# Float32 value products of two heads side by side in an attention stage, with row sums from GpSimd additions and quarter-array ones products

## The chip, the cores and the metric

The kernel runs on one core of a Trainium2 chip. The metric is device time in microseconds (us). Five engines work side by side, each executing its own instructions in order: TensorE (PE, with its weight loads shown as PEld), VectorE (DVE), ScalarE (ACT), GpSimd (POOL) and SyncE (SP, which here only issues transfers). They wait for one another through semaphores.

## The reference

One layer of a streaming encoder: modulation, a norm, one input projection, a depthwise convolution for half of the channels and attention with forget gates for the other half, an output projection, and a gated feed-forward network. There are 2048 prompt frames, and 8 sample streams of 16 frames with 1024 cached frames each. Everything is float32. The attention of the prompt, which the change is about, has 8 heads of 64 and is causal:

```python
def _attend(q, k, v, cum_q, cum_k, q_pos, k_pos):
    s = jnp.einsum('bqhd,bkhd->bhqk', q, k, preferred_element_type=jnp.float32) * (HEAD_DIM ** -0.5)
    s = s + (cum_q[..., :, None] - cum_k[..., None, :])
    mask = k_pos[None, :] <= q_pos[:, None]
    s = jnp.where(mask, s, NEG_INF)
    p = jax.nn.softmax(s, axis=-1)
    return jnp.einsum('bhqk,bkhd->bqhd', p.astype(v.dtype), v)
```

`cum` is the running sum of the log forget values. Queries and keys are normalized per head with large gains, so scores are large and need full float32 accuracy.

## The kernel before

The stages follow one another: input projection of the convolution's and the value's columns (to about 280 us), of queries and keys (to 578 us), the attention with the sample streams' attention woven in (to 1198 us), the output projection (to 1330 us), and the feed-forward network. Large products use fp32r, TensorE's fast reduced-precision form: an operand is split into a high part (ScalarE copies it to fp32r) and the remainder (VectorE or GpSimd subtracts), in `parts_of`, and three products high x high, low x high, high x low give the accuracy.

**Order.** A planner simulates the program and orders each engine's instructions by priority and simulated time. `later` shifts the priority of what is created within it (by `MAXIMA_BY` for the maxima, `BACK_BY` for the background). `after` pins an instruction behind another without a semaphore where both are on one engine. `weave` interleaves generators by the counts given with them.

**Steps.** `STEPS` goes over 4 pairs of heads and, for each, 4 blocks of 512 queries (`qb`). A step has `4 * qb + 4` key blocks of 128; the last four are on the diagonal and are cut to 512, 384, 256 and 128 queries. In all 320 score blocks (a key block, one head).

**A score block** (`attend`, L967 on): scores for 128 keys x 512 queries, transposed, are two fp32r products into one of three PSUM banks `u` (L973, L977): `K1`,`Q1` and `K2`,`Q2` hold the parts of the head's rows in the combinations needed; the second pair also has the gate sums and, in rows 96 to 103, the queries' maxima against -1, so that the product subtracts them. On the diagonal a third product adds the mask (L979). ScalarE takes the exponential into `ef` (L981). `parts_of` (L1160, L1161) splits it into the two parts of `e`; every third subtraction goes to GpSimd, the others to VectorE. The value product (L964) is three fp32r products per head into a bank of its own, of width 128: 64 columns of values and 64 columns of ones, so that the row sums come with it. At the end of a step ScalarE copies sums and values out (L998, L999), takes the inverse of the sums by logarithm and exponential, VectorE refines and multiplies (L1003 to L1005), and the result is stored in `cat_d`.

**Maxima** (`score_maxima`, L909 on): the exponential needs each query's maximum first. A product over 96 rows (L934, banks `cv`, two of them) gives the scores the other way round, VectorE reduces each block (L937), and `spread_maxima` (L945) transposes the result and writes it with the help of a mask `bm` into eight rows of `Q2` (L950). Maxima run ahead of the scores by 32 blocks and more; L974 and L975 pin it.

**Loads**: keys (L889, L891) and queries (L903, L927) by GpSimd's queue, values by SP's (L906), the latter split into two parts.

**Background** (`background`, from the third step on): the norm of the convolution's output (`conv_norm`), then `sample_setup` and eight `sample_batch`es. Their PSUM bank is `lane`; many of their products are plain float32 in column tiles of the array (`tile_position`): 32 columns each, four at a time.

## Time and profile before

| | us |
|---|---|
| median of 3 runs (2818.45 to 2822.88) | 2819.75 |
| the profiled execution | 2814.3 |
| its span, first to last instruction | 2812.5 |

Over the whole span the engines are busy: PE 2718.6 us (97%), DVE 2161.9 (77%), ACT 1428.7 (51%), POOL 503.9 (18%). TensorE's granted clock is 0.983 in the mean.

How to read the rows that follow: a row of groups gives line, engine, operation, output and inputs by tile name, rows x columns of the array for PE, the shape, the count, then busy time in us and the mean of one in ns, and the idle time of that engine ahead of them with what ended it. A timeline row starts with start and length in us; a float32 product appears as two instructions, an fp32r product as one. A row of waits has who waited for whom, the total in us, how often, and the longest. A stage row has the window, its length, then each engine's busy time with its count, the granted clock, the transfer engines' share and GB/s.

### The profile page before, as it was taken

The page shows a single profiled execution, that of the slowest core. Times are in us where ns is not written, and L with a number is a line of the kernel's source. Part 1 is how long each engine was busy: PE and PEld are TensorE (multiplying, and loading weights), DVE is VectorE, ACT ScalarE, POOL GpSimd, SP SyncE. Part 2 cuts the span into 40 slices and gives each one's busy share as a digit, 9 for nine tenths or more (in the row PEclk, how much of TensorE's full clock was granted, in tenths as well). Part 3 has the DMA queues.
Part 4 walks back from the last instruction along what each step waited for, and adds up shares of the span by engine and source line. Part 5 has one row for each costly group of instructions (what it writes and reads, how often), then busy time and mean ns, then how long its engine had stood idle before and what let it go on. Part 6 is the DMA issues. An engine that isn't in the chain of part 4 may idle for free. (4 is left out here: it accounts for less than half of the span.)

```text
span 2812.5 us, 48566 instructions
## 1 busy us (share of the span) xinstructions
PE 2718.6 (97%) x16536; PEld 2515.7 (89%) x16536; DVE 2161.9 (77%) x4235; ACT 1428.7 (51%) x2812; POOL 503.9 (18%) x685
## 2 busy tenths in 40 slices
PE   7999999999989999999999999999999999999999
PEld 6999988866667777698999989999999999999999
DVE  2798898989888787546397989877887778666765
ACT  4443323357776777744354446444554446555552
POOL 3454411243333222214201110000000000000000
PEclk9999999979999999999999999999999999999999
DMA  8753657673334766365576869866786769788883
GB/s 325 249 192 107 191 209 267 182 204 109 101 95 128 203 179 189 130 215 179 181 259 209 294 215 308 268 221 218 233 287 214 226 190 319 244 284 257 271 255 116
DMA packets 389960, 599.24 MB, mean 213 GB/s; under 512 B 47136, under 2 KB 250048, under 8 KB 387664
## 3 DMA queue, kind: packets, MB, share of 16 engines
q1 hardware_dynamic: 375248, 570.73, 62.8%
q0 software_dynamic: 14464, 25.42, 3.9%
q8 instruction: 130, 2.13, 0.3%
q14 instruction: 118, 0.97, 0.1%
HBM read 421.97 MB, written 174.08 MB: 212 GB/s over the span
## 5 line engine op out<-in xcount | busy, mean ns | idle before, releaser
L1456 PE MATMUL z<-rT,rW 128*128 128x360 f32 (+1 forms) x8316 | 1383.3, 328 | 5.5 <-ACT rW L1160 1.4
L1456 PEld LDWEIGHTS z<-rT,rW 128*128 128x128 f32 x8316 | 1378.7, 188 | 8.1 <-ACT rW L1160 2.4
L1160 ACT ACTIVATE rW<-rR 128x512 fp32r<-128x512 f32 x714 | 434.4, 617 | 386.8 <-PE z L1456 272.1
L1161 DVE TENSOR_TENSOR rW<-rR,rW 128x512 fp32r<-128x512 f32 x714 | 479.5, 676 | 154.5 <-ACT rW L1160 151.3
L700 DVE SCALAR_TENSOR_TENSOR cv<-cu,cpar,cv 128x384 f32<-128x384 f32 x580 | 311.6, 614 | 2.8 <-ACT cv L698 2.8
L964 PE MATMUL pv<-e,V 128*128 128x512 f32 (+3 forms) x960 | 268.9, 388 | 14.1 <-DVE e L1161 6.3
L964 PEld LDWEIGHTS pv<-e,V 128*128 128x128 f32 x960 | 167.9, 194 | 71.7 <-DVE e L1161 14.6
L937 DVE TENSOR_REDUCE M<-mx 128x1 f32<-128x512 f32 (+2 forms) x320 | 188.7, 603 | 50.2 <-PE mx L934 31.7
L981 ACT ACTIVATE ef<-s 128x512 f32<-128x512 f32 (+3 forms) x320 | 167.1, 532 | 116.7 <-PE s L979 47.1
L512 PE MATMUL z<-hqx,wqh 128*128 128x384 f32 (+1 forms) x768 | 196.6, 333 | 1.0 <-DVE logf L347 1.0
L1160 ACT ACTIVATE rT<-traw 128x360 fp32r<-128x360 f32 (+1 forms) x315 | 149.1, 501 | 91.7 <-DMA traw<-gt_d 62.9
L1161 DVE TENSOR_TENSOR rT<-traw,rT 128x360 fp32r<-128x360 f32 (+1 forms) x315 | 157.6, 531 | 45.0 <-ACT rT L1160 44.7
L1161 POOL TENSOR_TENSOR e<-ef,e 128x512 fp32r<-128x512 f32 (+3 forms) x106 | 127.2, 1200 | 347.4 <-ACT e L1160 180.7
L1160 ACT ACTIVATE e<-ef 128x512 fp32r<-128x512 f32 (+3 forms) x320 | 175.5, 567 | 4.0
L1161 DVE TENSOR_TENSOR e<-ef,e 128x512 fp32r<-128x512 f32 (+3 forms) x214 | 149.1, 704 | 35.4 <-ACT e L1160 34.4
L512 PEld LDWEIGHTS z<-hqx,wqh 128*128 128x128 f32 x768 | 135.7, 188 | 18.9 <-issue 15.3
L934 PE MATMUL mx<-K,Q 96*128 96x512 f32 (+2 forms) x320 | 134.3, 427 | 17.5 <-DVE M L937 11.3
L1144 PE MATMUL acc<-ch,woh 128*128 128x360 f32 (+1 forms) x384 | 127.4, 333 | 10.0 <-ACT ch L1160 4.6
L1384 DVE TENSOR_TENSOR rR<-rR 128x512 f32<-128x512 f32 (+1 forms) x136 | 93.4, 707 | 50.9 <-DMA rR<-w_down 44.1
L973 PE MATMUL s<-Q,K 128*128 128x512 f32 (+3 forms) x320 | 125.8, 393 | 3.4 <-ACT ef L981 3.4
L1144 PE MATMUL acc<-ch,wol 128*128 128x360 f32 (+1 forms) x384 | 126.9, 331 | 0.0
L512 PE MATMUL z<-hqx,wql 128*128 128x384 f32 (+1 forms) x384 | 126.4, 329 | 0.0
(306 smaller groups left out, 3935.4 us busy)
## 6 DMA issues: line engine op xcount, KB each, us to landing
rR<-sup_d SPq DMA_DIRECT2D x176, 256.0 KB
rR<-w_gate SPq DMA_DIRECT2D x132, 256.0 KB
traw<-gt_d SPq DMA_DIRECT2D x154, 180.0 KB
rR<-w_down SPq DMA_DIRECT2D x104, 256.0 KB
rR<-sdn_d SPq DMA_DIRECT2D x96, 256.0 KB
rR<-w_up SPq DMA_DIRECT2D x88, 256.0 KB
sup_d<-rR SPq DMA_DIRECT2D x88, 256.0 KB
wa<-w_ada SPq DMA_DIRECT2D x16, 1024.0 KB
```

The source lines that it names most:

```text
L512: nc.tensor.matmul(z[:, :n], w[:, m], x[:, :n], start=(c == 0 and k == 0), stop=(c == CB - 1 and k == 2))
L700: self.pin(nc.vector.scalar_tensor_tensor(dst, src, w, acc[i], ALU.mult, ALU.add))
L934: self.mx.append(nc.tensor.matmul(mx[:, :w], Q2[0:AUX, h, j * P:(j + 1) * P], K2[kb][0:AUX, h, :w], start=True, stop=not diag))
L937: nc.vector.tensor_reduce(M[:, i, kb:kb + 1], mx[:, :w], AX.X, ALU.max)
L964: nc.tensor.matmul(z[h][:, off:], V[kt // 4][:, v, kt % 4, h:h + 2, :].rearrange("p b c -> p (b c)"), e[:, x, off:], start=(kt == 0 and i ...
L973: first = nc.tensor.matmul(s[:, off:], K1[kb][:, h, sl], Q1[:, h, off:], start=True, stop=False)
L981: self.last_piece = nc.scalar.activation(ef[:, off:], s[:, off:], AF.Exp)
L1144: self.nc.tensor.matmul(z[:, :n], w[:, m], y, start=(first and i == 0 and k == 0), stop=(last and i == len(terms) - 1 and k == 2))
L1160: copy = self.nc.scalar.activation(hi, raw, AF.Copy)
L1161: engine.tensor_tensor(lo, raw, f32(hi), ALU.subtract)
L1384: nc.vector.tensor_tensor(t, x, y, op)
L1456: nc.tensor.matmul(z, W[:, x, m], t[:, y, :w], start=(k == 0 and i == 0), stop=(k == n - 1 and i == 2))
```

## The change

The attention's inner loop is written anew. The exponential `e` stays float32 and isn't split. Values stay float32 too. The two heads' value products are each one float32 product, 64 columns wide, at columns 0 and 64 of the array, into the two halves of one bank; they come two key blocks behind the scores, across steps. For full key blocks GpSimd adds the exponentials of two neighbouring blocks; products with a 32-column block of ones, on quarters of the array, sum what it adds (two heads x two halves of the list) into a second bank. On the diagonal the exponentials themselves are summed so. At the end of a step two ScalarE copies take values and sums out; the sums go through DRAM (`sum_d`) to be laid over 128 partitions, are inverted, go through DRAM again (`inv_d`) to be spread over the heads' rows, and one VectorE product divides. These four pieces are due 2, 6, 9 and 14 score blocks later. The last step does it with one product and a reciprocal of 512 columns.

Besides: pins on PE put the value products behind the scores and what follows behind the value products; background products are pinned behind the last score; loads of keys and queries go by SP's queue; the maxima fill one row of `Q2`, by eight transfers, and no mask; their priority is lower and their lead somewhat different; one Newton step less in two inverse roots; the sample streams' keys and biases are loaded earlier (`next_keys`, `next_bias`), with more pauses in the setup.

```diff
-MAXIMA_BY, BACK_BY = -300, 1000
+MAXIMA_BY, BACK_BY = 30, 1000
...
-            newton_rsqrt(nc, y, zp.tile([P, NB], F32, tag="t", name="rt", bufs=1)[:, :n], v, 2, self.pin)
+            newton_rsqrt(nc, y, zp.tile([P, NB], F32, tag="t", name="rt", bufs=1)[:, :n], v, 1, self.pin)
...
-                nc.tensor.matmul(pm[32 * j:32 * j + 32, :n], self.ones[:, 0:32], src[j], start=True, stop=True,
+                self.behind(nc.tensor.matmul)(pm[32 * j:32 * j + 32, :n], self.ones[:, 0:32], src[j], start=True, stop=True,
...
-            nc.gpsimd.dma_start(K2[0:HD + 2], rows[HD:])
+            nc.sync.dma_start(f32(K2[0:HD + 2]), rows[HD:])
...
-        nc.gpsimd.dma_start(Q1, self.q_d[2 * p:2 * p + 2, :, t].rearrange("h r t -> r h t"))
+        nc.sync.dma_start(f32(Q1), self.q_d[2 * p:2 * p + 2, :, t].rearrange("h r t -> r h t"))
...
-        raw = self.awk.tile([P, 4, P], F32, tag="rs", name="vraw", bufs=1)
-        v = self.Vt[n % 4]
+        v = self.Vt[n % 5]
+        nc.sync.dma_start(v, self.a["o_v"][t].rearrange("(t p) e -> p t e", p=P)[:, :, p * P:(p + 1) * P])
...
+                    if self.last_product:
+                        self.after(self.mx[-1], self.last_product)
...
-        for h in range(2):
-            nc.vector.tensor_tensor(Q2[r, h, :].rearrange("r (j q) -> r j q", j=4),
-                                    pz[r, :].unsqueeze(1).broadcast_to([8, 4, P]),
-                                    self.bm[r, h, :].unsqueeze(2).broadcast_to([8, 4, P]), ALU.mult)
+        m = self.lp.tile([P, P], F32R, tag="mrow", name="mrow", bufs=1)
+        nc.vector.tensor_copy(m[r], pz[r])
+        for i in range(8):
+            nc.sync.dma_start(f32(Q2[AUX:AUX + 1, i // 4, i % 4 * P:(i % 4 + 1) * P]), f32(m[AUX + i:AUX + i + 1]))
...
-        def value(kt, h, off, e):
-            for i, (v, x) in enumerate(((0, 0), (0, 1), (1, 0))):
-                nc.tensor.matmul(z[h][:, off:], V[kt // 4][:, v, kt % 4, h:h + 2, :].rearrange("p b c -> p (b c)"), e[:, x, off:],
-                                 start=(kt == 0 and i == 0), stop=(kt == nkt - 1 and i == 2))
+        def add_up(terms, last=False):
+            if terms and not started:
+                z.append(self.bank("tr", "sm"))
+            behind = self.last_product
+            for i, (g, o, x) in enumerate(terms):
+                self.last_product = nc.tensor.matmul(z[1][32 * g:32 * g + 32, o:], self.ones[:, 0:32], x[:, o:], start=(g not in started),
+                                                     stop=last and g not in [t[0] for t in terms[i + 1:]], tile_position=(0, 32 * g))
+                self.after(self.last_product, behind)
+                started.add(g)
+
+        def values(kt, off, es):
+            if kt == 0:
+                z.append(self.bank("tr", "pv"))
+            for h in range(2):
+                product = nc.tensor.matmul(z[0][HD * h:HD * h + HD, off:], V[kt // 4][:, kt % 4, HD * h:HD * h + HD], es[h][:, off:],
+                                           start=(kt == 0), stop=(kt == nkt - 1), tile_position=(0, HD * h))
+                if h == 0:
+                    self.after(product, self.last_s)
+            self.last_product = product
+            if kt < 4 * qb:
+                if kt % 2 == 0:
+                    for h in range(2):
+                        two = wk.tile([P, 512], F32, tag="two", name="two", bufs=6)
+                        nc.gpsimd.tensor_tensor(two, es[h], self.waiting[0][3][h], ALU.add)
+                        sums.append((2 * (kt // 2 % 2) + h, 0, two))
+                elif kt % 4 == 1:
+                    ready, sums[:] = sums[:-2], sums[-2:]
+                    add_up(ready)
+                return
+            sums.extend((2 * (kt % 2 if qb else 0) + h, off, es[h]) for h in range(2))
+            if kt % 2 == 0:
+                return
+            if kt == nkt - 1:
+                zc = wk.tile([P, 512], F32, tag="zc", name="zc")
+                self.last_exp = nc.scalar.copy(zc, z[0])
+            add_up(sums, kt == nkt - 1)
+            sums.clear()
+            if kt == nkt - 1:
+                self.end_of_step(p, qb, zc, z[1])
...
-                at = min(self.nscore + AHEAD + min(self.nscore // 6, 8), len(self.mx) - 1)
+                at = min(self.nscore + AHEAD + min(self.nscore // 5, 10), len(self.mx) - 1)
                 self.after(first, self.mx[at])
+                if self.last_product:
+                    self.after(first, self.last_product)
...
-                self.parts_of(e[:, 0, off:], e[:, 1, off:], ef[:, off:], nc.gpsimd if self.split3 == 0 else nc.vector)
+                e = wk.tile([P, 512], F32, tag="e", name="e", bufs=12)
+                self.last_piece = nc.scalar.activation(e[:, off:], s[:, off:], AF.Exp)
+                es.append(e)
+                if h:
+                    self.waiting.append((values, kt, off, es))
+                    if len(self.waiting) > 2:
+                        self.next_values()
+                while self.due and self.nscore >= self.due[0][0]:
+                    self.due.pop(0)[1]()
...
+    def end_of_step(self, p, qb, zc, sums):
+        sm = wk.tile([P, 512], F32, tag="sm", name="sm", bufs=1)
+        self.last_exp = nc.scalar.copy(sm[r], sums[r])
...
+        for i in range(2 * parts):
+            nc.sync.dma_start(self.sum_d[p, qb, i:i + 1], sm[32 * i:32 * i + 1])
+        w = wk.tile([P, 2, 2, 4], F32, tag="inv", name="inv")
+        def load():
+            nc.sync.dma_start(w[:, 0:parts], self.sum_d[p, qb, 0:2 * parts].rearrange("(k h) (a c) -> a k h c", h=2, c=4))
+        def invert():
+            if qb:
+                self.after(nc.vector.tensor_tensor(w[:, 0], w[:, 0], w[:, 1], ALU.add), self.last_max)
+            self.after(nc.vector.reciprocal(w[:, 0], w[:, 0]), self.last_max)
+            nc.sync.dma_start(self.inv_d[p, qb].rearrange("h (a c) -> a h c", c=4), w[:, 0])
+        def back():
+            for h in range(2):
+                nc.sync.dma_start(R[HD * h:HD * h + HD], self.inv_d[p, qb, h:h + 1].broadcast_to([HD, 512]))
+        def divide():
+            self.after(nc.vector.tensor_tensor(zc, zc, R, ALU.mult), self.last_max)
+            nc.sync.dma_start(cat, zc)
+        self.due += [(self.nscore + k, f) for k, f in ((2, load), (6, invert), (9, back), (14, divide))]
+
+    def behind(self, op):
+        def issue(*args, **kw):
+            ins = op(*args, **kw)
+            self.after(ins, self.last_s)
+            return ins
+        return issue
```

More of the change, by code (lines that the diff above doesn't have):

```diff
@@ L800, in attention @@
         first = self.load(0)
-        next(first)
-        next(first)
+        drain(first)
         for n, (p, qb) in enumerate(STEPS):
@@ L860, in background @@
         bank = self.bank("ss", "lane")
-        more = self.after_attention.enter_context(self.pool(name="e2", bufs=1, side="right"))
-        self.eslots += [(more, f"e{i}") for i in range(5, 8)]
         with self.pool(name="cn", bufs=1) as cn:
@@ L986, in attend @@
-                self.parts_of(e[:, 0, off:], e[:, 1, off:], ef[:, off:], nc.gpsimd if self.split3 == 0 else nc.vector)
-                waiting.append((kt, h, off, e))
-                if h and len(waiting) > len(self.eslots) - 3:
-                    value(*waiting.pop(0))
-                    value(*waiting.pop(0))
-                yield
-        for w in waiting:
-            value(*w)
-        pvs, sm = (wk.tile([P, 512], F32, tag=k, name=k, bufs=1) for k in ("pvs", "sm"))
-        for h in range(2):
-            o, x = slice(HD * h, HD * h + HD), slice(HD - HD * h, P - HD * h)
-            nc.scalar.copy(sm[o], z[h][x])
-            nc.scalar.copy(pvs[o], z[h][o])
@@ new lines, in attend, with next_values @@
+        if n + 1 == len(STEPS):
+            while self.waiting:
+                self.next_values()
+    def next_values(self):
+        values, *x = self.waiting.pop(0)
+        values(*x)
+    def end_of_step(self, p, qb, zc, sums):
+        nc, wk = self.nc, self.awk
+        parts = 2 if qb else 1
+        r = slice(0, 64 * parts)
+        sm = wk.tile([P, 512], F32, tag="sm", name="sm", bufs=1)
+        self.last_exp = nc.scalar.copy(sm[r], sums[r])
+        cat = self.cat_d[:, 4 + p, qb * 512:(qb + 1) * 512]
+        R = wk.tile([P, 512], F32, tag="R", name="aR", bufs=1)
+        if (p, qb) == STEPS[-1]:
+            spread = self.bank("cv", "R")
+            nc.tensor.matmul(spread, self.four, sm, start=True, stop=True)
+            nc.vector.reciprocal(R, spread)
+            nc.vector.tensor_tensor(zc, zc, R, ALU.mult)
+            nc.sync.dma_start(cat, zc)
+            return
+        for i in range(2 * parts):
[13 more added lines that the diff above has]
+            self.after(nc.vector.tensor_tensor(zc, zc, R, ALU.mult), self.last_max)
+            nc.sync.dma_start(cat, zc)
+        self.due += [(self.nscore + k, f) for k, f in ((2, load), (6, invert), (9, back), (14, divide))]
@@ L1014, in sample_setup @@
         self.catS = sm.tile([P, NP, NS, QS], F32, name="catS")
+        lf = self.smc.tile([P, 8, NS * H], F32, tag="kc", name="lfc")
+        nc.sync.dma_start(lf, a["clfT"])
+        tri = sm.tile([P, 4, P], F32, tag="pT", name="tri2", bufs=2)[:, 0]
+        nc.sync.dma_start(tri, a["tri_s"])
+        sel = sm.tile([P, NS + QS], F32, name="sel")
+        nc.sync.dma_start(sel, a["sel"])
         nc.sync.dma_start(self.maskS, a["maskS"])
```

125 lines of the change are left out of this document (61 added, 64 removed).

## The prediction

> **What bounds the kernel now.** I read the stage table first, since the change touches only the middle of the kernel.
>
> ```profile
> core 0: us, PE busy (x) PEld busy (x) DVE busy (x) ACT busy (x) POOL busy (x), PEclk, DMA share, GB/s
> 280.00:578.00 298.00, 295.99 (x1844) 256.57 (x1842) 270.82 (x643) 95.62 (x201) 82.25 (x115) 1.00 0.66 212
> 578.00:634.00 56.00, 51.30 (x227) 36.70 (x227) 48.10 (x106) 26.24 (x55) 25.29 (x30) 0.70 0.80 204
> 634.00:1198.00 564.00, 525.24 (x3102) 390.59 (x3100) 448.07 (x773) 416.08 (x836) 162.23 (x156) 0.97 0.49 141
> 1330.00:2812.00 1482.00, 1465.58 (x8835) 1461.47 (x8833) 1133.58 (x2203) 710.11 (x1389) 60.69 (x53) 1.00 0.75 242
> ```
>
> The attention takes 634 to 1198 us. TensorE (PE) reads 93% busy there, VectorE (DVE) 79%, ScalarE (ACT) 74%. The stage behind it keeps PE at 99%, so whatever the attention saves or loses moves the end by the same amount. But a busy PE isn't a PE at its peak: a matmul's bar holds its drain as well as its turn. Turns are read from starts in the timeline. The next rows hold a plain run, a product of four 32-column tiles in plain float32, a 64-column one, and a float32 product on the whole array.
>
> ```profile
> 969.11 0.39 PE L973 MATMUL s<-Q,K 128*128 128x512 f32 x1
> 969.34 0.39 PE L977 MATMUL s<-Q,K 128*128 128x512 f32 x1
> 969.65 1.06 PE L1073 MATMUL lane<-kc,Qbd 128*32 128x512 f32 x8
> 970.65 0.50 PE L973 MATMUL s<-Q,K 128*128 128x512 f32 x1
> 970.99 0.39 PE L977 MATMUL s<-Q,K 128*128 128x512 f32 x1
> ...
> 909.52 0.22 PE L979 MATMUL s<-masks 128*128 128x128 f32 x1
> 909.67 1.09 PE L1038 MATMUL lane<-tri,lfc 128*64 128x128 f32 x8
> 910.69 1.19 PE L964 MATMUL pv<-e,V 128*128 128x512 f32 x4
> ...
> 725.52 1.02 PE L721 MATMUL lane<-cm,mean 128*128 128x512 f32 x2
> 725.98 0.79 PE L934 MATMUL mx<-K,Q 96*128 96x512 f32 x1
> 726.61 0.63 PE L964 MATMUL pv<-e,V 128*128 128x512 f32 x2
> ```
>
> A reduced-precision (fp32r) product of 512 columns takes a turn of 0.23 us (from 969.11 to 969.34). A float32 product is two instructions, and from 725.52 to 726.61 it and one fp32r product take 1.09 us, so it takes about 0.85. Four float32 products in 32-column tiles go in one such slot: from the score product at 969.34 to that at 970.99 lie 1.65 us, of which two ordinary turns are 0.46. So the visit costs 1.19 us, 0.34 over its 0.85, for going into the tiled form and coming back. The 64-column row shows it on entering too: 909.52 to 909.67 is 0.15 us, where a quarter of 0.23, the turn of its 128 columns, is 0.06.
>
> What PE must do in these 564 us, by turns. Of the 320 score blocks 224 are 512 wide (three value products each, x672) and 32 each are 384, 256 and 128 by the causal triangle, together 272 widths of 512.
>
> ```profile
> L964 PE MATMUL pv<-e,V 128*128 128x512 f32 x672 | 210.4, 419 | 9.4 <-DVE e L1161 5.2 <-ACT e L1160 2.2 <-POOL e L1161 1.7
> ...
> L936 PE MATMUL mx<-masks 128*128 128x128 f32 x108 | 25.7, 238 | 0.0
> ...
> 634.00:1198.00 564.00, 121.72 (x391) 72.29 (x391) 168.37 (x284) 0.97 0.49 141
> ...
> 634.00:1198.00 564.00, 86.02 (x982) 37.60 (x982) 24.15 (x63) 19.23 (x39) 0.97 0.49 141
> ```
>
> The last two rows are the stage table for the maxima's bank (`mx`) and for the background's (`lane`). Values: 3 x 272 x 0.23 = 188 us. Scores: 2 x 272 x 0.23 = 125. Maxima: of the 391 instructions 108 are masks, so 283 of the 320 products fall in this stage: 272 x 283/320 x 0.23 = 55. Masks: 108 and the scores' 124, 232 x 0.06 = 14. Background: 86 busy, about 80 in turns. Together 462. The other 102 us are waits and the slowed clock (3% of 564 is 17). So the stage is limited by PE and its waits, and the waits are these:
>
> ```profile
> PEld mx L934 <- DVE M L937: 19.8, 28, 1.8
> PEld pv L964 <- DVE e L1161: 14.6, 25, 1.3
> ...
> PEld pv L964 <- ACT e L1160: 8.5, 16, 1.6
> PEld pv L964 <- POOL e L1161: 6.9, 10, 1.5
> ...
> PE mx L934 <- DVE M L937: 8.8, 11, 1.5
> PE pv L964 <- DVE e L1161: 6.3, 13, 1.1
> ...
> PE pv L964 <- POOL e L1161: 3.6, 7, 1.2
> PE pv L964 <- ACT e L1160: 3.6, 6, 1.2
> ```
>
> **The change, part by part.**
>
> *Value products.* Six fp32r products per key block (two heads, three each) become two float32 ones side by side in 64-column tiles. A block of full width then takes one visit, 1.19 us, for 6 x 0.23 = 1.38. All of them: 136 widths x 0.85 = 116, and 160 visits x 0.34 = 54, so 170 for 188. No row has two 64-column tiles side by side. Bounds: as the four 32-column tiles of the row at 969.65 (0.85 for both), or one after the other as two products like that at 725.52 (1.70, 116 us more). I take the first, since that row is the same kind of tile.
>
> The page "TensorE: Matmul & The Clock Gate" of the Trainium skill (Part 3, measured speedup) gives three column tiles 2.38 times, not 3 times. Taken over to two tiles at the same efficiency, an estimate from that page, that would be 1.59 times and about 30 us more for the values. The trace speaks against it: the four tiles' visit shows no more than its 0.34 over one product, so by that rule the time would be 2810, and I leave it inside the rival on tiles below.
>
> *Row sums.* The ones columns leave the value product, and come back as four quarter-array products. The 96 pairs of full blocks' exponentials (both heads) make 24 groups x 0.85 = 20. The diagonal's 128 terms: in the 12 steps with qb > 0, two groups of 0.85 and 0.43, 15 us; in the 4 with qb = 0 the two blocks share quarters and go in turn, 4 x 2.13 = 9. These 44 visits stand behind value products that are tiled already. Each changes from 64 to 32 columns, between 0 and 0.34; I take 0.15, as on entering at 909.52, 7 us. Sums: 51. PE thus has 221 us for 188, 33 more work.
>
> *Background behind the scores.* Its tiled products are pinned after the last score, beside the values, and may share a visit: 0 to 13 us less (some 66 visits x 0.2); I take 5. So PE needs 462 + 33 - 5 = 490.
>
> *The split of the exponentials goes.* That is where the gain must come from:
>
> ```profile
> L1160 ACT ACTIVATE e<-ef 128x512 fp32r<-128x512 f32 (+3 forms) x316 | 173.2, 567 | 4.0
> L1161 DVE TENSOR_TENSOR e<-ef,e 128x512 fp32r<-128x512 f32 (+3 forms) x212 | 147.2, 701 | 35.4 <-ACT e L1160 34.4
> L998 ACT COPY sm<-pv 64x512 f32<-64x512 f32 x31 | 18.0, 581 | 5.6 <-PE pv L964 4.9
> L1004 DVE SCALAR_TENSOR_TENSOR sm<-sm,rs 128x512 f32<-128x512 f32 x15 | 12.8, 850 | 0.0
> ```
>
> ACT falls from 416 to about 200, DVE from 448 to about 250 (also without the three end-of-step operations and with one full-width divide in their place). The waits on `e`, 14.6 + 8.5 + 6.9 + 6.3 + 3.6 + 3.6 = 43.5, go: a value product now comes two blocks after its exponential. The waits of maxima on DVE, 28.6, should halve with DVE's load: 14 less. Fewer waits let the clock keep up: 9 of its 17. What is left is 102 - 43.5 - 14 - 9 = 36 (bounds: 10, the clock's rest alone, and 102, nothing better). The stage then takes 490 + 36 = 526, 38 less than 564.
>
> *GpSimd (POOL).* It does 96 additions of 128x512.
>
> ```profile
> L1161 POOL TENSOR_TENSOR e<-ef,e 128x512 fp32r<-128x512 f32 x74 | 98.7, 1334 | 267.6 <-ACT e L1160 132.2 <-issue 40.3 <-PE pv L964 27.9
> L1161 POOL TENSOR_TENSOR e<-ef,e 128x512 fp32r<-128x512 f32 (+3 forms) x105 | 126.2, 1202 | 347.4 <-ACT e L1160 180.7 <-issue 48.6 <-PE pv L964 27.9
> ```
>
> 96 x 1.33 = 128 us, as the 126 that go. Two per two blocks, 2.7 us in some 6.6; a sum is used three blocks later, so they are hidden. If that cover went, each of 48 pairs would cost up to 2.7.
>
> *End of a step.* Row sums go through DRAM to be inverted, four transfers in a chain, off PE's path unless DVE comes to its inversion or division early (a rival below). *Keys, queries and the maxima rows* move to SP's queue, and with the ends of steps give it 64 + 128 + 127 more issues.
>
> ```profile
> 1196.63 1.85 SPq L1196 DMA_DIRECT2D cr<-cat_d  x4
> ...
> SPq L906 <- DVE sm L1004: 166.2, 12, 30.5
> ...
> SPq L711 <- DMA cat_d<-cy: 16.3, 4, 6.7
> ...
> Q<-q_d POOLq DMA_DIRECT2D x14, 512.0 KB, 5.3
> ```
>
> 319 x 0.46 = 147 us of issuing in 526. The longest wait there today, for a value buffer (166.2), goes with the buffer. The cover is the lead of maxima (32 blocks or more) and one step for queries; I count 0. A queue that falls behind by more than a step's lead would cost its delay in full. *Priority and lead of maxima*: no work; hidden by that lead.
>
> *One Newton step less.* Ahead of 578 PE is busy 295.99 of 298, so nothing. In the tail 578 to 634 two blocks each lose three operations:
>
> ```profile
> 594.87 0.55 DVE L94 SCALAR_TENSOR_TENSOR rt<-ry 128x384 f32<-128x384 f32 x1
> ...
> 596.04 0.56 DVE L96 SCALAR_TENSOR_TENSOR ry<-rt,ry 128x384 f32<-128x384 f32 x1
> ```
>
> 1.7 us a block (the last is narrower); I take 2 in all.
>
> **Sum.** The profiled execution took 2814.3 us (span 2812.5 and 1.8 around it). 2814.3 - 38 - 2 = 2774.3. The runs' median is 2819.75, 5.5 above the profiled one, so 2780 on its scale.
>
> **The rivals.**
>
> 1. *Waits vanish almost wholly* and the background shares its visits: 462 + 33 - 13 + 10 = 492, 72 less, 2745 with the tail. For it: ACT and DVE at half load. Against: the background's own chain (product, copy, product) still stops an in-order PE.
>
> 2. *Waits stay*, because PE's order is now fixed by pins: at 70 us of waits the stage takes 560 and nothing is won, some 2814. For it: only 43.5 of 102 us name the split.
>
> 3. *The inversion stops DVE: slower.* DVE executes in order; behind the inversion stand the maxima's reductions, and for these waits the `mx` product, and all of PE behind it. The chain from the end of a step: a copy 0.6, four stores 4 x 0.46, write-then-read 4.1 (16.3/4), landing 5.3 (the nearest row, though a large transfer): 11.8 us. The inversion is due after 6 scores, 3 blocks of 526/160 = 3.3 us, 9.9. It is 1.9 late, and two maxima banks give PE about one block, 3.3, of slack. With the longest write-then-read (6.7) it is 4.5 late, 1.2 past the slack; with both round trips and the division's so, 15 steps x (1.2 + 3.4) = 69, so 2780 + 69 = 2849. It decides from 40/15 = 2.7 us past the slack per step.
>
> The page "DMA: Bandwidth & Descriptors" of the Trainium skill (Anatomy of one DMA) gives a small transfer a fixed 2.0 us. By that the chain would be 0.6 + 1.8 + 2 x 2.0 = 6.4 us and in time; the rows here are slower, so the rival keeps its chance.
>
> 4. *Tiles of 64 columns don't overlap*: up to 116 us more, 2896; half of that 2838. For it: no row shows them. Against: the row at 969.65.
>
> **How the numbers follow.** Forecast 0.52 (its own range 2762 to 2797, waits of 18 to 53 us); rival 1 0.14; rival 2 0.12; rival 3 0.14; rival 4 0.08. What a measurement here can tell from no change is 0.2%, 5.6 us. Faster: 0.52 + 0.14 + some 0.05 of rivals 2 and 4, 0.71; the same 0.09; slower 0.20. The range 2738 to 2840 leaves out most of rivals 3 and 4.
>
> **What would show it.** Starts of value products: a visit of about 1.2 us for a full block (near 2.0: rival 4). PE work by turns about 30 us more, with 30 to 40 us of waits for 102. ACT near 200 and DVE near 250 busy. DVE waiting on a transfer ahead of the inversion, and `mx` products on DVE, is rival 3. Clock in the stage at 0.98 or better. The stages from the output projection on unchanged. The forecast is wrong if the stage takes over 550 us, or if it shrinks while the value products don't change as said.

## The result, and the profile after

| | kernel before | changed kernel |
|---|---|---|
| median of the runs, us | 2819.34 (2818.45 to 2822.88, 4 runs) | 2802.26 (2799.87 to 2804.06, 4 runs) |
| profiled execution, us | 2814.3 | 2804.06 |
| its span, us | 2812.5 | 2802.3 |

The ratio is 0.9935, with a 95% interval of 0.9919 to 0.9951: the change makes the kernel 18 us faster by the ratio (17 by the medians), where 40 were forecast. The profiled executions differ by 10.2 us only, since that of before lies 5.0 below its median and that of after 1.8 above.

The busy time of each engine on the changed kernel's page:

```profile
PE 2719.9 (97%) x16666; PEld 2388.6 (85%) x16666; DVE 1975.1 (70%) x3951; ACT 1237.1 (44%) x2406; POOL 461.2 (16%) x616
```

The changed kernel between the same bounds as the attention has in the prediction: length, then busy time and instructions of PE, PEld, DVE, ACT and POOL, the granted clock, the DMA engines' share, GB/s.

```profile
634.00:1198.00 564.00, 537.08 (x3183) 272.74 (x3183) 282.03 (x514) 235.87 (x453) 130.31 (x100) 0.97 0.52 152
```

ScalarE and VectorE lost most of what was said (236 and 282 us are left, for 200 and 250), but the clock of the stage is 0.97 and not the 0.98 that was to show the waits gone. Where the time went is seen from the places at which the timeline starts its first and last products of a kind (the projection's products run until 1407 us in the kernel before; the 1330 given with its stages above is too early):

| us from the span's start | before | after |
|---|---|---|
| first score product | 624.6 | 621.4 |
| last value product | 1197.6 | 1176.2 |
| first product of the output projection | 1200.5 | 1187.2 |
| first product of the stage behind it | 1407.2 | 1399.9 |
| end | 2812.5 | 2802.3 |

So the attention itself is 18.2 us shorter (573.0, now 554.8). Of this 8.1 are given back between the last value product and the projection (2.9, now 11.0), and 6.0 within the projection (206.7, now 212.7). The stages behind are 2.9 shorter, and the scores begin 3.2 sooner.

The value products do what was forecast. The changed kernel's timeline, PE only (start, duration, engine, line, operation; "x4" are two heads of two passes each):

```profile
1033.74 0.22 PE L1012 MATMUL s<-masks 128*128 128x128 f32 x1
1033.89 1.08 PE L971 MATMUL pv<-e,V 128*64 128x512 f32 x4
1034.90 0.50 PE L923 MATMUL mx<-K,Q 96*128 96x512 f32 x1
1035.24 0.34 PE L1004 MATMUL s<-Q,K 128*128 128x384 f32 x1
```

From the end of the mask product's turn (1033.80, at 0.06 us) to the maxima product are 1.10 us, and that product's own turn is 0.34 for 0.23: 1.21 us for the visit. The two 64-column tiles run side by side.

What does not agree are PE's waits. The waits of PE from 620 to 1300 us in the changed kernel: total, times, longest.

```profile
PE mx L923 <- DVE M L928: 9.7, 9, 3.2
PE lane L1074 <- DVE S L1175: 5.1, 2, 3.0
PE lane L1189 <- ACT S L1182: 3.2, 1, 3.2
PE pv L971 <- ACT zc L991: 3.0, 1, 3.0
PE mx L923 <- DVE suf L1112: 2.8, 1, 2.8
PE acc L1244 <- DVE xo L1252: 2.6, 1, 2.6
PE lane L1074 <- DMA cy<-y_d: 2.3, 1, 2.3
```

No wait of the value products on their exponentials is left here, but nearly every row stands for single stops of 2 to 3 us. The prediction had also counted the waits of the weight loads (PEld). These overlap PE's work, so they aren't lost time by themselves. In the same view for PEld the maxima's wait, which was to halve, is 47.3 us for 19.8 in the kernel before, and loads of the scores still wait for exponentials:

```profile
PEld mx L923 <- DVE M L928: 47.3, 52, 4.0
PEld s L1004 <- ACT e L1014: 12.1, 18, 0.8
```

I count all stops of PE as follows, for each kernel below in the same way: a matmul's turn is the time to the next one's start; what goes beyond the lower quartile of the same pair of shapes is a stop, and stretches at half clock are set apart. Until the last value product the kernel before has 467 us of turns, 90 of stops and 19 lost to the clock (some 3 of the stops lie behind that product). The changed kernel has 491, 49 and 16. Turns +24 (forecast +28), stops and clock -44 (forecast -66).

The split into turns and stops depends on what counts as the same pair. A finer count, which also tells the tiles apart, gives 473, 83 and 17 before, and 486, 54 and 15 after. So differences of some 10 us in these sums, and of a few us below, are not to be trusted; that fewer stops went than forecast holds in both counts.

### The profile page after: what moved, and what is told of

Its sections match the earlier page's. It is cut to its first block, busy times and chain, and to the rows that moved or that the text cites. A ratio compares the mean times of both kernels' runs of the same rounds, so it can differ in the third digit from the quotient of the medians.

```text
span 2802.3 us, 48143 instructions
## 1 busy us (share of the span) xinstructions
PE 2719.9 (97%) x16666; PEld 2388.6 (85%) x16666; DVE 1975.1 (70%) x3951; ACT 1237.1 (44%) x2406; POOL 461.2 (16%) x616
## 5 line engine op out<-in xcount | busy, mean ns | idle before, releaser
L1014 ACT ACTIVATE e<-s 128x512 f32<-128x512 f32 (+3 forms) x320 | 168.4, 533 | 278.2 <-PE s L1012 140.2
L980 POOL TENSOR_TENSOR two<-e 128x512 f32<-128x512 f32 x96 | 127.2, 1342 | 398.3 <-ACT e L1014 328.0
L923 PEld LDWEIGHTS mx<-K,Q 96*128 96x128 f32 x320 | 63.7, 201 | 116.6 <-DVE M L928 54.7
L923 PE MATMUL mx<-K,Q 96*128 96x512 f32 (+2 forms) x320 | 145.2, 463 | 17.1 <-DVE M L928 12.6
L971 PE MATMUL pv<-e,V 128*64 128x512 f32 (+3 forms) x640 | 156.6, 565 | 3.0 <-ACT zc L991 3.0
L514 PEld LDWEIGHTS z<-hqx,wqh 128*128 128x128 f32 x768 | 136.0, 188 | 16.6 <-issue 12.4
L1004 PE MATMUL s<-Q,K 128*128 128x512 f32 (+3 forms) x320 | 127.6, 399 | 0.0
L1244 PE MATMUL acc<-cl,woh 128*128 128x360 f32 (+1 forms) x384 | 122.3, 331 | 0.0
L1010 PE MATMUL s<-Q,K 128*128 128x512 f32 (+3 forms) x320 | 119.3, 373 | 0.0
```

The lines of the kernel that those rows point to most:

```text
L514: nc.tensor.matmul(z[:, :n], w[:, m], x[:, :n], start=(c == 0 and k == 0), stop=(c == CB - 1 and k == 2))
L923: self.mx.append(nc.tensor.matmul(mx[:, :w], Q2[0:AUX, h, j * P:(j + 1) * P], K2[kb][0:AUX, h, :w], start=True, stop=not diag))
L971: product = nc.tensor.matmul(z[0][HD * h:HD * h + HD, off:], V[kt // 4][:, kt % 4, HD * h:HD * h + HD], es[h][:, off:], start=(kt == 0), s ...
L980: nc.gpsimd.tensor_tensor(two, es[h], self.waiting[0][3][h], ALU.add)
L1004: first = nc.tensor.matmul(s[:, off:], K1[kb][:, h, sl], Q1[:, h, off:], start=True, stop=False)
L1014: self.last_piece = nc.scalar.activation(e[:, off:], s[:, off:], AF.Exp)
```

## The experiments

All ratios are to the kernel before, measured beside it on the same chip. The experiments ran on several chips, so gains from one to another are taken from the ratios and not from the times.

**1. The background sooner.** In the changed kernel the last batch of the sample stream ends behind the attention, at 1204 us.

```
-MAXIMA_BY, BACK_BY = 30, 1000
+MAXIMA_BY, BACK_BY = 30, 150
```

> Edit: the background (the sample batches and the convolution's normalization) is put 150 places behind the attention in the planner's order and not 1000, so that its eighth batch is issued some eight value visits ahead of the last one. Theory A (the missing gain lies in the last batch, which spills past the last value product: the gap to the output projection grew from 2.9 to 11.0 us and the projection by 6): gap back to about 3 us, projection back to about 207, the attention itself longer by what was moved into its idle places, in all 2802 - 12 = 2790 us (2786 to 2795). Rival B (TensorE has no idle places left, the moved work only lengthens the attention by as much): the gap closes, the attention grows by 10 to 14 us, 2798 to 2804 us. Rival C (background work met sooner waits more often for VectorE): 2805 us or more.

Measured: ratio 0.9895 (0.9880 to 0.9911), 2785.73 us, 11 us better than the changed kernel by the ratios. The time is about theory A's (2785.73 us lies just below its range; by the ratio to 2819.34 it is 2789.7), and the reason it gave is not. The gap is still 10.5 us, and now PE stands in it. The waits of PE from 1160 to 1175 us, and the timeline there:

```profile
PE acc L1244 <- ACT ch L1260: 7.9, 1, 7.9
```

```profile
1161.84 1.12 PE L1043 MATMUL R<-sm,four 128*128 128x512 f32 x2 [0.72 <-ACT sm L1038]
1163.00 3.36 DVE L1044 RECIPROCAL aR<-R 128x512 f32<-128x512 f32 x1 [24.38 <-PE R L1043]
1166.46 0.69 DVE L1045 TENSOR_TENSOR zc<-zc,aR 128x512 f32<-128x512 f32 x1
1167.18 0.32 SPq L1046 DMA_DIRECT2D cat_d<-zc  x1
1167.60 1.82 SPq L1296 DMA_DIRECT2D cr<-cat_d  x4
...
1170.84 0.67 PE L1244 MATMUL acc<-ch,woh 128*128 128x368 f32 x1 [7.87 <-ACT ch L1260]
```

The last step divides on the spot: row sums, a product that spreads them, a reciprocal of 3.36 us, the division, a store. SP issues in order, and behind this store stand the projection's first loads, which need none of it. In the kernel before they were issued at 1196.63 (the prediction's row of `cr<-cat_d`), before that kernel's last value product.

What the edit gained lies in the attention: 542.6 us for 554.8. Its turns are 486 for 491, though the eighth batch, 11 us of turns behind the attention until now, lies inside it; stops are 51 for 49, the clock's loss 7 for 16. All of the background's products together cost 62 us of turns, for 72 in the changed kernel. More of the batch's 32-column products may stand in visits that the values open anyway, but experiment 7 gains nearly as much where there are no such visits, so this isn't shown to be the reason.

**2. The last store on another queue,** alone and together with the first edit.

```
             nc.vector.tensor_tensor(zc, zc, R, ALU.mult)
-            nc.sync.dma_start(cat, zc)
+            nc.gpsimd.dma_start(cat, zc)
             return
```

> Edit, on the changed kernel alone: the store of the last step's result (cat_d<-zc) is issued by GpSimd's queue and not by SyncE's, where the output projection's first loads (cr<-cat_d) stand right behind it and wait, with it, for the reciprocal of 3.36 us and the division. Theory A (that queue, and not the eighth batch's products, sets the gap of 11.0 us between the last value product and the first product of the projection; moving the batch ahead left a gap of 10.5 us in which TensorE stood still for 8.2): gap 3 to 5 us, what is left of the eighth batch moves into the projection, 4 to 7 us faster than the changed kernel, ratio to the kernel before 0.991 to 0.992. Rival B (the eighth batch's products and TensorE's slowed clock behind them set the gap): gap 9 to 11 us, ratio 0.9935 as measured.

> Edit: the background 150 places behind and the last store on GpSimd's queue, both. Theory A: the stall of 8.2 us ahead of the projection goes, and with it the slowed clock of 10.2 us that followed it (5 us): gap 2 to 4 us, 8 to 12 us faster than the first edit alone, ratio to the kernel before 0.985 to 0.987. Rival B (the projection's first loads wait for something else, for instance the space of their buffers, until about the same time): gap 8 us or more, ratio 0.989 to 0.990.

Measured: alone 0.9946 (0.9929 to 0.9962), which is the changed kernel's ratio; with the first edit 0.9872 (0.9857 to 0.9887), just above theory A's 0.985 to 0.987. Alone, the loads go out at 1175.36, but the gap is 12.7 us: in PE's order the eighth batch's products stand ahead of the projection's, and they wait for VectorE, that is, for the same reciprocal. The kernel with this edit alone, waits of PE from 1172 to 1186 us:

```profile
PE lane L1189 <- ACT S L1182: 3.2, 1, 3.2
PE lane L1074 <- DVE S L1175: 3.0, 1, 3.0
```

With both edits the gap is 3.4 us and the reciprocal runs beside the projection:

```profile
1165.80 1.27 SPq L1296 DMA_DIRECT2D cr<-cat_d  x3
1165.81 3.36 DVE L1044 RECIPROCAL aR<-R 128x512 f32<-128x512 f32 x1 [24.38 <-PE R L1043]
...
1166.46 0.43 PE L1244 MATMUL acc<-ch,woh 128*128 128x368 f32 x1 [0.69 <-ACT ch L1260]
```

So the 11 us had two causes in parallel, the queue and the late batch, and either one is enough. My expectation for the edit alone took the first to be the only one. The longer projection isn't explained by this: it takes 208.0 us with the background sooner and 211.4 with both edits, for 212.7 in the changed kernel and 206.7 before. The clock in the gap follows. Ten microseconds of each kernel, first with the background sooner only, then with both (the column ahead of the DMA share is the clock):

```profile
1165.00:1175.00 10.00, 4.16 (x14) 4.16 (x15) 4.00 (x6) 2.49 (x5) 0.00 (x0) 0.50 0.64 197
```

```profile
1165.00:1175.00 10.00, 8.18 (x44) 7.11 (x43) 6.74 (x7) 5.04 (x9) 0.64 (x1) 1.00 0.67 211
```

**3. Later divisions.** VectorE comes to a step's division before the inverted sums are back. It waits in the changed kernel, in the kernel with both edits above, and with both and the pairs of experiment 4:

```profile
DVE zc L1066 <- DMA aR<-inv_d: 16.5, 5, 6.5
```

```profile
DVE zc L1066 <- DMA aR<-inv_d: 30.3, 10, 6.1
```

```profile
DVE zc L1067 <- DMA aR<-inv_d: 41.7, 10, 9.7
```

```
-        ... ((2, load), (6, invert), (9, back), (14, divide))]
+        ... ((3, load), (8, invert), (13, back), (20, divide))]
```

> Edit, on the changed kernel alone: the division's parts due 3, 8, 13 and 20 scores after a step's end in place of 2, 6, 9 and 14. Theory A (early divisions stop VectorE 16.5 us there, and a part of TensorE's 50 us of stalls stands behind it): 3 to 7 us faster than the changed kernel, ratio to the kernel before 0.9905 to 0.9925. Rival B (in the changed kernel these waits fall into VectorE's slack; they count only once the background comes earlier): 0.993 to 0.995. Rival C (a later division holds the copy of the next value products, which found its buffer not yet stored once already, 3.1 us): 0.995 or more.

> Edit: background 150 places behind, last store on GpSimd's queue, and the four parts of a step's division due 3, 8, 13 and 20 scores after its end in place of 2, 6, 9 and 14. Theory A (third rival of the prediction in small: VectorE stands 30 us, ten times, before the division, waiting for aR<-inv_d, and each time the maxima's reductions and with them TensorE's maxima products stand behind it): VectorE's waits there fall below 10 us, TensorE's stalls on the maxima from 23 to some 17, ratio to the kernel before 0.9845 to 0.986. Rival B (VectorE's waits there fall into its own slack, the maxima wait for something else): the ratio of the same kernel without this, 0.987 within 0.0015.

Measured: on the changed kernel alone 0.9927 (0.9912 to 0.9942), no difference that can be told; on top of both edits 0.9855 (0.9833 to 0.9877) for 0.9872, in theory A's range, but the intervals overlap, and the lower end of rival B's range is the same 0.9855. VectorE's wait falls to 12.4 us there, not below the 10 that theory A named, and PE's stops to 45 us from 53 in one profiled execution of each. Whether time was won stays open.

```profile
DVE zc L1066 <- DMA aR<-inv_d: 12.4, 4, 3.9
```

**4. Two key blocks in one visit.**

```
-                    if len(self.waiting) > 2:
+                    if len(self.waiting) > 3:
+                        self.next_values()
                         self.next_values()
```

> Edit: the value products of two key blocks are issued one right behind the other (four 64-column products in one visit), so 80 visits in place of 160; the number of products is the same. Theory A (a tiled visit costs 0.34 us for entering and leaving, whatever it holds): 80 x 0.34 = 27 us of TensorE less, of which shared visits and the longer distance between score products give some back: 20 us faster than the changed kernel, 2782 us (2775 to 2790). Rival B (what TensorE saves turns into waits, because ScalarE and VectorE find fewer score products to work on during a visit of two microseconds): 2798 to 2810 us, waits on the maxima and on the exponentials grow by about as much as the products shrink.

> Edit: as the second run of these, with the value products of two key blocks in one visit. In the run of pairs alone TensorE's own need fell by 22 us (27 by the count of visits), waits grew by 13 to 16 and the gap by 2. Theory A (part of these waits were the late background's, which is gone here): 6 to 14 us faster than the second run, ratio 0.981 to 0.984. Rival B (longer visits starve VectorE of maxima and ScalarE of scores whatever the background does): ratio 0.985 to 0.988, waits 12 us and more above the second run's.

> Edit: the same, with the value products of two key blocks in one visit. Without the later division the pairs lost their 23 us of TensorE's need to 17 us more of stalls, the longest one (8.0 us) behind a VectorE that waited 9.7 us for aR<-inv_d. Theory A (that wait is what eats the pairs' gain): stalls fall from 70 to 58 us or less, ratio 0.982 to 0.9845. Rival B (a two microsecond visit makes maxima and scores wait whatever the division does): ratio 0.986 to 0.988.

Measured: alone 0.9944 (0.9926 to 0.9961), no gain; with both edits of 1 and 2 0.9872 (0.9845 to 0.9899), no gain; with the later division 0.9833 (0.9818 to 0.9848), 2772.37 us. The turns fell each time, by 22, 23 and 23 us (27 from 80 visits at 0.34). The stops took it back, 63 for 49, then 70 for 53; with the later division they are 67. Rival B was right of the first two. In the second the longest stop, 8.0 us, stands behind VectorE's 9.7 us wait for the division:

```profile
PE mx L923 <- DVE M L928: 21.9, 16, 7.8
```

With the division later the maxima's row is 12.4 us in 14 waits, the longest 2.2. The ratio is theory A's, but its sign, stops of 58 us or less, did not come. The rest of the stops stay above those of the same kernels without pairs: scores wait 23 us for 19, the background's products 18 for 12. That a pair's long visit leaves ScalarE and VectorE too little to work on would explain it; no run shows it by itself.

**5. No additions on GpSimd.** Ones products sum every exponential.

```
-                if kt % 2 == 0:
-                    for h in range(2):
-                        two = wk.tile(...)
-                        nc.gpsimd.tensor_tensor(two, es[h], self.waiting[0][3][h], ALU.add)
...
+                sums.extend((2 * (kt % 2) + h, 0, es[h]) for h in range(2))
+                if kt % 2:
+                    add_up(sums)
+                    sums.clear()
                 return
```

> Edit: GpSimd's 96 additions are left out, ones products sum every exponential: 96 more of them, in 24 more groups of four. Theory A (the additions hide and cost VectorE little): TensorE pays 24 x 1.0 = 24 us more, and some 5 us of waits go away with the stretched VectorE products, 2821 us (2815 to 2826). Rival B (GpSimd's additions, by stretching VectorE's two-operand products from 0.66 to 1.03 us in the normalization, are what keeps the waits at 45 and not 30 us): 24 us more and 15 to 20 us of waits less, 2804 to 2811 us.

Measured: 0.9998 (0.9985 to 1.0011), 18 us behind the changed kernel, in theory A's range (0.9998 of 2819.34 is 2818.8). The additions are worth their place, but they are not free. VectorE's products of the normalization in the changed kernel (busy us, mean ns), and without the additions:

```profile
L734 DVE TENSOR_TENSOR cy<-cy,cmu 128x512 f32<-128x512 f32 (+1 forms) x20 | 19.4, 1029 | 0.0
L749 DVE TENSOR_TENSOR cy<-cy,cr 128x512 f32<-128x512 f32 (+1 forms) x20 | 15.1, 815 | 0.0
```

```profile
L734 DVE TENSOR_TENSOR cy<-cy,cmu 128x512 f32<-128x512 f32 (+1 forms) x20 | 10.9, 603 | 0.0
L749 DVE TENSOR_TENSOR cy<-cy,cr 128x512 f32<-128x512 f32 (+1 forms) x20 | 10.9, 602 | 0.0
```

The Trainium skill, page "SBUF — State Buffer", section "SBUF: two separate sides", says that a VectorE operation with two inputs in SBUF and a GpSimd operation exclude each other for a whole instruction; the 1029 ns beside 603 agree. Each time the maxima's reductions come behind such a block of four:

```profile
686.08 3.57 DVE L749 TENSOR_TENSOR cy<-cy,cr 128x512 f32<-128x512 f32 x4
...
687.53 3.24 POOL L980 TENSOR_TENSOR two<-e 128x512 f32<-128x512 f32 x2 [5.41 <-PE sm L960]
...
690.30 0.39 PE L923 MATMUL mx<-K,Q 96*128 96x256 f32 x1 [1.62 <-DVE M L928]
```

By turns, the kernel without additions has 28 us more of them in the attention, 11 less of stops and 10 less lost to the clock. That would make 7 us in all and not 18; the profiled execution, 2812.03 us, lies 4 below the median, and its stages behind the attention take 4.6 longer. So theory B's mechanism is there, at more than the 5 us that theory A allowed it, and still smaller than what the additions save. The length of the blocks isn't shown to be the cause: with the four products broken into twos (below) the stops ahead of the maxima's products stay at 23 us in the finer count, while without the additions they are 13 for 20.

**6. The parts that were counted as 0,** each undone alone on the changed kernel: the maxima's place in the order (`MAXIMA_BY` -300 again), the loads of keys and queries (`nc.gpsimd.dma_start` again), the order that holds the background's products next to the values (the `after` in `behind` left out).

> Edit, on the changed kernel alone: the maxima's place in the planner's order as before (300 places ahead, not 30 behind). The prediction counted this part of the change as 0. Theory A: it is 0, ratio as the changed kernel's, 0.992 to 0.995. Rival B (maxima placed sooner wait less for VectorE): 0.989 to 0.9915. Rival C (they crowd TensorE and hold scores and exponentials back): 0.9955 or more.

> Edit, on the changed kernel alone: the loads of keys and queries go through GpSimd's queue again, as in the kernel before; the rows of the maxima stay on SyncE's. The prediction counted their place as 0. Theory A: 0, ratio 0.992 to 0.995. Rival B (on SyncE's queue they and the transfers of the division hold each other up): waits for aR<-inv_d fall below 10 us and the ratio is 0.9905 to 0.992. Rival C (GpSimd's additions hold the loads back, or the loads the additions): 0.9955 or more.

> Edit, on the changed kernel alone: the background's products lose the order that places them behind the newest score product, next to the value products. Theory A (this is what lets them share a tiled visit; 80 us of background at 0.34 us an entry): 4 to 8 us slower, ratio 0.995 to 0.9965. Rival B (the planner puts them into the same places without it): 0.9925 to 0.9945. Rival C (the order makes them wait, and without it they fill TensorE's waits): 0.992 or less.

Measured: 0.9976 (0.9962 to 0.9991), 1.0000 (0.9986 to 1.0014) and 0.9950 (0.9933 to 0.9967). The third lies at the edge of theory A, but its interval overlaps with the changed kernel's. The other two were not 0 at all; both lie in the range of their rival C.

With the maxima first, the attention is no slower (551.9 us until its last value product), so rival C's reason, held-back scores, isn't seen. The background is later still, and the projection's stage takes 220.9 us for 212.7, with 17 us at half clock for 10. How these 8 us come of the maxima's place stays open.

With the loads on GpSimd's queue the whole gain is gone. Scores begin at 627.1 for 621.4, the attention takes 563.9 for 554.8. GpSimd's idle time in this kernel, by what it waited for:

```profile
POOL two L980 <- ACT e L1014: 156.0, 36, 15.3
POOL Q L896 <- PE s L1012: 136.5, 14, 15.9
POOL K L884 <- PE s L1010: 31.2, 8, 7.0
```

A load of queries that waits for its buffer (up to 15.9 us) holds up the additions behind it; an addition that waits for an exponential holds up the loads. The stops of the background's products grow from 13 to 21 us. The longest, 6.1 us, ends when a bias row lands:

```profile
917.82 12.54 SPq L1148 DMA_DIRECT2D S<-bias_d  x15
...
929.88 0.69 DVE L1175 TENSOR_TENSOR S<-S,lane 128x512 f32<-128x512 f32 x1 [11.05 <-DMA S<-bias_d]
...
930.62 1.93 PE L1074 MATMUL lane<-kc,Qbd 128*32 128x512 f32 x8 [6.05 <-DVE S L1175]
```

How GpSimd's queue makes SP's row of loads late isn't seen in these lines, and I leave it open. That GpSimd's place for these loads costs 18 us is measured.

**7. The background sooner in the kernel before** (`BACK_BY` 150).

> Edit, on the kernel before: only the background's place, 150 behind and not 1000. Theory A (what the earlier background gained in the changed kernel, 11 us, came of its 32-column products lying in one visit with the 64-column value products, which the kernel before cannot share, and of a spilled batch that it does not have): ratio 0.9985 to 1.0015. Rival B (it came of smoother waits of any kind): ratio 0.994 to 0.997.

Measured: 0.9968 (0.9955 to 0.9981), 9 us, rival B. In the kernel before no product of the background can share a visit, and it has no spilled batch; a sooner background still helps, by nearly the 11 us that it won in the changed kernel. Shared visits and the spilled batch therefore aren't needed to explain that gain. The profiled execution, 2813.1 us of span, isn't faster than that of before, so where these 9 us lie isn't known.

**Without effect or slower.**

> Edit: a third buffer for the copied value products (in place of the twelfth of the exponentials), so that ScalarE's copy at a step's end need not wait until the division of the step but one before is stored. Theory A (that wait stopped TensorE once, for 3.1 us, and ScalarE's copy for 4.5 us): 2798 to 2801 us. Rival B (a late division costs more than the one stall seen, since each wait of ScalarE delays the exponentials behind it): 2790 to 2796 us. Rival C (the twelfth buffer of the exponentials was needed): slower than 2804 us.

> Edit: as the run before, and VectorE's blocks of four products in the convolution's normalization are broken after the second, so that reductions of the maxima come between. Theory A (TensorE's waits on the maxima, 19 to 22 us, lie behind such blocks, which take 3.6 to 4.6 us where GpSimd adds beside them): stalls on the maxima fall by 4 to 8 us, ratio lower by 0.001 to 0.003 than of the run before. Rival B (the waits come of VectorE's whole load and only move): the same ratio within 0.001.

> Edit: the fastest kernel so far (earlier background, last store on GpSimd's queue, pairs, later division; ratio 0.9833) with the maxima 120 places behind, not 30. Theory A (the place goes on paying as from 300 ahead to 30 behind, 11 us): ratio 0.979 to 0.982. Rival B (the order that each score waits for its maxima leaves them no more room): 0.9825 to 0.985. Rival C (maxima too late stop the scores): 0.986 or more.

A third `zc` for the twelfth `e`: 0.9966 (0.9955 to 0.9977), rival C; its profiled execution took 2799.17 us, 7 below the median, and doesn't show why. VectorE's products of the normalization in twos: 0.9872 (0.9847 to 0.9898), the same as without. The maxima 120 places behind in the kernel of pairs: 0.9936 (0.9913 to 0.9959) for 0.9833, rival C. So 30 is better than 300 ahead in the changed kernel and better than 120 behind in this one; what lies between wasn't tried.

**The versions that beat both.** Edits 1 and 2 with the later division: 2778.7 us, 0.9855; with pairs besides, 2772.37 us, 0.9833. The first of these by stretches, the attention with its gap and all behind it:

```profile
617.30:1158.50 541.20, 524.79 (x3256) 267.56 (x3255) 275.67 (x519) 233.33 (x454) 131.72 (x104) 0.98 0.53 156
1158.50:2770.90 1612.40, 1589.94 (x9564) 1582.56 (x9564) 1198.03 (x2321) 768.32 (x1498) 98.95 (x91) 0.99 0.73 238
```

From the first score to the projection are 541.2 us for 575.9 before, 34.7 less, and the rest is as before (1612.4 for 1612.0). That comes near the 38 of the forecast, but with three more edits, one of which wins 9 us in the kernel before as well. So most of the forecast gain can be reached with this inner loop in another order; that the change itself held all of it isn't shown.

## Why the prediction was wrong, point by point

**The step that failed** is this one: "What is left is 102 - 43.5 - 14 - 9 = 36 [...]. The stage then takes 490 + 36 = 526". By turns, 65 us of stops and lost clock are left, not 36 (69 in the finer count). The 43.5 of waits on `e` did go: ahead of the value products the finer count has 40 us of stops before and 3 after. The sum's 43.5 fits this partly by luck, since it adds rows of PEld and PE that overlap. The 14 for the maxima did not come: the stops ahead of their products are 20 us in both kernels, and PE's own row is 9.7 us for 8.8, though VectorE is less busy. The stops ahead of the scores grew, from some 18 to some 24. The 9 of the clock came to 3: its loss fell from 19 us to 16 and not to 8, since each stop of 1.6 us or more has half clock beside it.

The sum treated waits as single items that vanish with their cause. The changed kernel's timeline has others in their place: maxima's reductions behind four VectorE products beside GpSimd's additions, a copy that waits for a store, convolution outputs and bias values that come late. None lasts over 3.3 us. Why the maxima's stops did not halve is shown in part only, by experiment 5. Rival 2 named this outcome, 70 us of waits, and came nearest to the mechanism. It took the pins to be the cause. Without the background's pin (experiment 6) the time is no better; the other pins were not tried.

**"The stage behind it keeps PE at 99%, so whatever the attention saves or loses moves the end by the same amount"** failed too: of the attention's 18 us, 8 were lost in the gap behind it and 6 in the projection. Experiments 1 and 2 show the cause of the 8, not of the 6. I had priced the fifteen divisions through DRAM and not the sixteenth, which stands in line with the projection's loads, nor the background, whose last batch is placed behind a TensorE that the plan holds to be full. Against the forecast of 2774.3 for the profiled execution, 2804.06 is 29.8 more: 20 in the attention, 8 in the gap, 6 in the projection, less 3 in the stages behind and 1 in a start sooner than said.

**The PE work** was about right. A visit 1.21 us (forecast 1.19), turns +24 in the attention (+28), sums 50 (51); with the 11 us of turns that spilled, +35. In the finer count the turns are +13, and +24 with the spilled ones. Rival 4, tiles one after the other, is refuted by the row at 1033.89. With it falls the estimate after the Trainium skill's page "TensorE: Matmul & The Clock Gate" (Part 3), 30 us more for the values: here the trace shows no such loss for two tiles of 64 columns.

**ScalarE and VectorE**: 236 and 282 us busy for 200 and 250. The window up to 1198 now holds 11 us of the projection, and VectorE's products are stretched; I had left out both. Up to the projection's first product they are 228 and 277 us, so the window makes 8 and 5 of it.

**GpSimd**: 96 additions took 127.2 us, forecast 128. "They are hidden" holds for GpSimd; for VectorE it doesn't. Still, the additions save more than they cost (experiment 5).

**The counts of 0.** The key and query loads on SP's queue were worth 18 us, as much as the whole result, and the maxima's place 12. That both are gains was luck. I had asked whether SP could carry 319 more issues, and not what GpSimd's queue would suffer if it kept them beside the additions. The parts don't add up (18 and 12 against a total of 18): each was measured with the others in place.

**Rival 3**, division or inversion ahead of its data: VectorE waited for the division 16.5 us, for the inversion 0.2, and in the changed kernel this costs nothing that can be told. With both edits and pairs it is 41.7 us, and there the later division brought 0.9872 to 0.9833. The inversion was in time, but not as either estimate has it. The load of the sums is issued 2.7 to 14.5 us after their copy starts, since SP's queue also waits for other things, and the inversion runs 6.7 to 27.2 us after that start, where the prediction put it at 9.9. So these 0.2 us do not confirm the 6.4 us chain estimated after the page "DMA: Bandwidth & Descriptors" of the Trainium skill (Anatomy of one DMA); that section is also on transfers issued by GpSimd, and these go by SP. The division, two transfers later, was late five times, by up to 6.5 us.

**The start** was 3.2 us sooner (forecast 2).

## What to carry to other kernels

When a change frees an engine, don't subtract the waits that name it and call the rest the new time: list what each in-order queue will meet next, the queues that only issue transfers too, and count moved issues by what they stand behind and who stands behind them. Look at the last step by itself, since it has no next step to hide in; here, a 3.36 us reciprocal with a store in front of another stage's loads cost about a third of the change's gain, once the late batch was out of the way (0.9895 to 0.9872). If a large saving shows up small, first ask whether late work has moved past the stage's end.

## What the runs showed of the hardware

A stop of TensorE can cost more than its length. Behind the 1.6 us wait that ends at 690.3 the clock falls to half. The changed kernel, four stretches in a row:

```profile
684.00:688.40 4.40, 4.40 (x24) 2.12 (x24) 4.13 (x7) 1.19 (x2) 0.87 (x1) 1.00 0.00 0
688.50:691.00 2.50, 0.88 (x6) 0.65 (x5) 2.50 (x7) 0.60 (x1) 2.27 (x2) 1.00 0.16 63
691.60:695.00 3.40, 3.40 (x12) 2.08 (x8) 0.56 (x1) 0.91 (x2) 0.00 (x0) 0.51 0.60 198
695.10:700.00 4.90, 4.90 (x29) 2.98 (x29) 2.22 (x6) 1.26 (x3) 0.00 (x0) 1.00 0.60 193
```

The page "TensorE: Matmul & The Clock Gate" of the Trainium skill (Part 1) gives a window of about 3.4 us for this, and half clock after an idle window. The length agrees (3.4 us here, some 10 behind the 7.9 us stop of experiment 1); but here a stop of 1.6 us was enough. In the changed kernel's attention the seven stops of 1.6 us or more, and no other place behind the first value product, have half clock beside them, 3.4 us six times and 6.8 once. Two single stops of 1.5 us in the kernel before (at 808.0 and 1045.0) have none.

A reciprocal of 128x512 on VectorE takes 3.36 us, where a product of that size takes 0.69. Two groups of VectorE products with both inputs in SBUF took 1029 and 815 ns in the mean in the kernel with GpSimd's additions, for 603 and 602 without them.
